# Row halves, fixed turns and an earlier pool mix in a macaron block with RWKV-7 and pooling

## The chip, the cores and the metric

The kernel runs on one core of one Trainium2 chip. TensorE (PE) multiplies matrices into PSUM, VectorE (DVE), ScalarE (ACT) and GpSimd (POOL) work elementwise, SyncE (SP) and POOL issue DMA transfers. Every engine works through its own queue in order and waits for others on semaphores. The metric is the device time of one execution in microseconds (us): the median of three runs was 2127.09, from 2125.59 to 2128.98. A difference of about 0.2% can be told from none.

## What is computed

One block on 256 tokens of width 2048, in float32, with about 400 MB of weights that are read once:

```python
def _swiglu(x, w_gate, w_up, w_down):
    return (jax.nn.silu(x @ w_gate) * (x @ w_up)) @ w_down

f = _swiglu(_rmsnorm(h, ln_ffn1_pre[l]), ffn1_gate[l], ffn1_up[l], ffn1_down[l])
h = h + MACARON_WEIGHT * _rmsnorm(f, ln_ffn1_post[l])
mx = _hybrid_mixer(_rmsnorm(h, ln_mix_pre[l]), ...)
h = h + _rmsnorm(mx, ln_mix_post[l])
f = _swiglu(_rmsnorm(h, ln_ffn2_pre[l]), ffn2_gate[l], ffn2_up[l], ffn2_down[l])
h = h + MACARON_WEIGHT * _rmsnorm(f, ln_ffn2_post[l])
```

The hidden width of both feed-forwards is 5632. The mixer multiplies by w_in, runs an RWKV-7 scan over 16 heads on one part of the result and four causal pooling windows (each followed by a 256 x 256 matrix, the "mix") on another, gates the two projected branches with sigmoids of the rest, and multiplies the sum by w_out.

## The kernel before

**Products.** Each float32 operand is split into a high and a low float32r part, and a product is three matmuls: high x high, high x low, low x high (`mm3`, lines 117 to 121). Activations are the stationary operand, 128 x 128 for one k-tile and one of two row halves (h = 0, 1: tokens 0 to 127, 128 to 255); weights are the moving operand, 512 columns wide. `load_w` (line 87) fetches two k-tiles of weights per DMA (512 KB, issued by SP), ACT casts them to the high part wH (L101), and DVE subtracts to get the low part wL (L102). There are four buffers for raw weights and five each for wH and wL, so weights run at most five pairs of k-tiles ahead.

**`gemm_tok`** (line 123) makes 512 columns of a product: normally for each k-tile both row halves in turn, each into its own PSUM bank, then the evacuation `evac(h, ps)`. With `lead` the first 10 k-tiles (STAG) go by row halves: all ten for h = 0, then all ten for h = 1. With `trail` the last 10 do, and each half is evacuated when it ends. The product that starts a stage is a lead, the last column block of a stage is a trail.

**`post`** (line 295) ends a stage: four column blocks of the down or output product. Each block's evacuation takes the sum of squares on ACT (L267) and multiplies by the norm's gain on DVE (L314). After the last block the sum is finished (L327), POOL raises it to the power -0.5 (L330), and DVE scales each of the four column blocks and adds the residual (L335, one step per row half and column block). Each finished block goes to `emit`, which stores it (a spill to DRAM by POOL, or the output by SP) and, between stages, calls the `emit` of `next_pre` (line 346): four PE transposes (L234), their split into xH on ACT (L240) and xL on DVE (L241) as the next stage's input, the block's sum of squares for the next norm (L267), and after four blocks the row's factor (`rstd`, L214 to L219).

**Order.** Tile, the framework, plans each engine's queue ahead of time, by simulated times and a priority that follows the program's order; `high_priority(offset)` moves instructions forward by so many places. Weight casts and most evacuations stand in `high_priority(offset=BOOST)`, 2000. Inside `manual_schedule(engines={PE})` PE takes its instructions exactly as the program gives them. Before the change only the mixer's middle part does so (line 578): there `weave` puts the scan's steps among the matmuls of the projections (`rest`), by estimated times (MM, MC: us per matmul).

**The pool branch.** `p_g` (line 519) makes four window products and the mix of each one window later; then a gate product of 32 steps (`gb_g(1)`, one step is a k-tile and a row half), and after it the mix of the fourth window (`pool_mix(3, ...)`). The window's evacuation ends with mxT, the input of the mix (L625 high, L626 low part); the mix's evacuation gives yb (L638 high, L639 low part), of which the projection `pb_g(0)` needs the fourth for its last two k-tiles.

**Buffers.** 33 units of 4 KB per partition hold activations. At the end of a feed-forward 22 of them are its hidden activations (hT), two are gains (gb), four the result (fg), four the residual; the next input takes eight. A unit comes free after its last reader.

Of the kernel before, what the change touches and what calls it, by code (L numbers as in the profile page):

```python
# [10 lines left out]
F32R = mybir.dt.float32r  # L11
# [5 lines left out]
P = 128  # L17
# [15 lines left out]
W32_BUFS = 4  # L33
WS_BUFS = 5
BOOST = 2000
MM, MC = 0.2265, 0.12
NUNITS = 33
STAG = 10
TB = 4

ROWS = [("ln_mix_pre", 16), ("ln_ffn2_pre", 16), ("mu", 26), ("w0", 8), ("a0", 8),
# [4 lines left out]
class Block:  # L46
    def __init__(s, tc, ctx):
        s.tc = tc
        s.nc = nc = tc.nc
        E = ctx.enter_context  # L50
        s.n = 0
        s.cp = E(tc.tile_pool(name="cp", bufs=1))
        s.wp = E(tc.tile_pool(name="wp", bufs=3))
        s.up = E(tc.tile_pool(name="up", bufs=NUNITS))
        s.tp = E(tc.tile_pool(name="tp", bufs=TB))
        s.sp = E(tc.tile_pool(name="sp", bufs=4))
        s.dp = E(tc.tile_pool(name="dp", bufs=1, space=bass.MemoryType.DRAM))
        s.pm = E(tc.tile_pool(name="pm", bufs=4, space=PSUM))
        s.pt = E(tc.tile_pool(name="pt", bufs=4, space=PSUM))
        s.ident = s.const([P, P], "ident")  # L60
        make_identity(nc, s.ident)
        s.mhalf = s.const([P, 16], "mhalf")
        nc.gpsimd.memset(s.mhalf, -0.5)
# [20 lines left out]
    def psum(s, p="pt"):  # L84
        return s.pt.tile([P, 512], F32, tag="pt", name=s.nm(p))

    def load_w(s, w, k0, nk, c0, cw, split=False):
        nc = s.nc
        out = []
        step = 1 if split else max(1, 1024 // cw)  # L90
        for j in range(k0, k0 + nk, step):
            n = min(step, k0 + nk - j)
            w32 = s.wp.tile([P, 1024], F32, tag="w32", name=s.nm("w32"), bufs=W32_BUFS)
            wH = s.wp.tile([P, 1024], F32R, tag="wH", name=s.nm("wH"), bufs=WS_BUFS)
            wL = s.wp.tile([P, 1024], F32R, tag="wL", name=s.nm("wL"), bufs=WS_BUFS)
            v, vH, vL = [t[:, :n * cw].rearrange("p (k c) -> p k c", k=n)
                         for t in (w32, wH, wL)]
            nc.sync.dma_start(out=v, in_=w[j * P:(j + n) * P, c0:c0 + cw]
                              .rearrange("(k p) c -> p k c", p=P))
            with s.tc.high_priority(offset=BOOST):  # L100
                nc.scalar.copy(vH, v)  # L101
                nc.vector.tensor_tensor(out=vL, in0=v, in1=vH.bitcast(F32), op=ALU.subtract)  # L102
            for i in range(n):
                out.append((j + i, vH[:, i], vL[:, i]))
        return out
# [17 lines left out]
    def gemm_tok(s, w, c0, at, KT, evac, lead=False, trail=False, first=False):  # L123
        pss = [s.pm.tile([P, 512], F32, tag="mm", name=s.nm("mm")) for _ in range(2)]

        def do(k, wH, wL, h):
            xH, xL = at(k)
            s.mm3(pss[h], xH[:, h * P:h * P + P], xL[:, h * P:h * P + P], wH, wL,
                  k == 0, k == KT - 1)

        k0 = 0
        while k0 < KT:
            nk = 4
            if lead and k0 == 0 or trail and k0 + STAG == KT:
                nk = STAG
            elif trail and KT - STAG - k0 < 4:
                nk = max(KT - STAG - k0, 2)
            nk = min(nk, KT - k0)
            stag = (lead and k0 == 0) or (trail and k0 + nk == KT)
            ws = []  # L140
            for k1 in range(k0, k0 + nk, 4):
                ws += s.load_w(w, k1, min(4, k0 + nk - k1), c0, 512, first and k1 == 0)
                if not stag:
                    for k, wH, wL in ws:
                        do(k, wH, wL, 0)
                        do(k, wH, wL, 1)
                    ws = []
            if stag:
                for h in range(2):
                    for k, wH, wL in ws:  # L150
                        do(k, wH, wL, h)
                    if k0 + nk == KT:
                        evac(h, pss[h])
            k0 += nk
        if not trail:
            with s.tc.high_priority(offset=BOOST):
                for h in range(2):
                    evac(h, pss[h])

    def tok_g(s, w, c0, at, KT, evac):  # L160

# [133 lines left out]
    def post(s, wd, at, KT, gpost, fac, resid, emit, reload):  # L295
        nc = s.nc
        gb = [s.unit(p="gb") for _ in range(2)]
        fg = [[s.unit(p="fg") for _ in range(2)] for _ in range(2)]
        ss = [s.small(4, "ss") for _ in range(2)]

        def cc_(u, c):
            return u[c // 2][:, (c % 2) * 512:(c % 2) * 512 + 512]

        part = [None, None]
        rr = [None, None]
        kf = 1.0 / (D * fac ** 2)

        for c in range(4):
            def ev(h, ps):
                if h == 0 and c % 2 == 0:  # L310
                    nc.gpsimd.dma_start(out=gb[c // 2], in_=gpost[c * 512:c * 512 + 1024]  # L311
                                        .partition_broadcast(P))
                s.sumsq(ps, ss[h][:, c:c + 1])
                nc.vector.tensor_tensor(out=cc_(fg[h], c), in0=ps, in1=cc_(gb, c), op=ALU.mult)  # L314
                if c == 2 and h == 0:
                    reload()
                if c == 2:
# [9 lines left out]
                nc.vector.tensor_scalar(out=r2, in0=ss[h][:, 3:4], scalar1=kf,  # L327
                                        scalar2=part[h], op0=ALU.mult, op1=ALU.add)
                r = s.small(1, "rs", bufs=8)
                nc.gpsimd.tensor_tensor(out=r, in0=r2, in1=s.mhalf[:, :1], op=ALU.pow)  # L330
                rr[h] = r
                for hh, q in ([(0, 0), (0, 1)] if h == 0 else
                              [(1, 0), (1, 1), (0, 2), (0, 3), (1, 2), (1, 3)]):
                    o = cc_(fg[hh], q)
                    nc.vector.scalar_tensor_tensor(out=o, in0=o, scalar=rr[hh],  # L335
                                                   in1=resid(hh, q), op0=ALU.mult,
                                                   op1=ALU.add)
                    emit(hh, q, o)
            s.gemm_tok(wd, c * 512, at, KT, ev, trail=(c == 3))

    def next_pre(s, gT):
        uT = s.new_T(4)
        ss = [s.small(4, "ss2") for _ in range(2)]
        rs = [None, None]

        def emit(h, c, ap):
            s.transpose_split(ap, uT, c, h, gT)
            s.sumsq(ap, ss[h][:, c:c + 1])
            if c == 3:
                rs[h] = s.rstd(ss[h], D)  # L350
        return uT, rs, emit

    def setup_mixer(s, prm):
# [73 lines left out]
    def mixer(s, prm, uT, rs, resid, emit, gpost, reload):  # L427
# [91 lines left out]
        def p_g():  # L519
            mix = None  # L520
            for g, win in enumerate(POOL_WINDOWS):
                mxT = s.unit((P, 2, 2, S), F32R, "mxT")
                yield from s.pool_window(g, win, at, w_in, mxT)
                if g:
                    yield from s.pool_mix(g - 1, mix, prm["pool_w"], pT)
                mix = mxT
            yield None
            yield from gb_g(1)
            yield from s.pool_mix(3, mix, prm["pool_w"], pT)

        sga = []

# [456 lines left out]
def kernel(tc, x, ln_ffn1_pre, ln_ffn1_post, ffn1_gate, ffn1_up, ffn1_down,  # L989
# [11 lines left out]
    with ExitStack() as ctx:  # L1001
# [3 lines left out]
        def at_tok(u):  # L1005
            return lambda h, c: u[h][c // 2][:, (c % 2) * 512:(c % 2) * 512 + 512]
# [25 lines left out]
            return f  # L1032
        hsp = s.dp.tile([2, 2, P, D], F32, tag="hsp", name="hsp")

        def emit1(h, c, ap):
            pre2(h, c, ap)
# [7 lines left out]
        def emit2(h, c, ap):  # L1044
            pre3(h, c, ap)
# [4 lines left out]
        def emit(h, c, ap):  # L1050
            nc.sync.dma_start(out=out[0, h * P:h * P + P, c * 512:c * 512 + 512], in_=ap)
        s.ffn(ffn2_gate[0], ffn2_up[0], ffn2_down[0], uT3, rs3, ln_ffn2_post[0],
              at_tok(h2), emit, load_to(h2, lambda h: hsp[1, h]))


_INS = ["x", "ln_ffn1_pre", "ln_ffn1_post", "ffn1_gate", "ffn1_up", "ffn1_down", "ln_mix_pre",
# [29 lines left out]
```

## Time and profile before

| what | us |
|---|---|
| median of three runs | 2127.09 |
| the profiled execution's own time | 2125.91 |
| its span, first to last instruction | 2124.2 |
| PE busy | 2093.8 |
| DVE busy | 1257.3 |
| ACT busy | 1115.9 |
| POOL busy | 77.7 |

The profile shows the first feed-forward until about 735 us, the mixer until about 1386 us, and the second feed-forward. Its rows give a start in us from the span's start, a duration, the engine, the line (L102 is line 102 of the kernel), the operation, output and inputs, shapes and a count; in square brackets stands the idle time before it and what ended that. Matmuls are pipelined, so the start of the next row tells more than a matmul's own duration. The granted clock is the share of TensorE's full clock that its throttle let through.

### The profile page before, as it was taken

The page shows a single profiled execution, that of the slowest core. Times are in us where ns is not written, and L with a number is a line of the kernel's source. Part 1 is how long each engine was busy: PE and PEld are TensorE (multiplying, and loading weights), DVE is VectorE, ACT ScalarE, POOL GpSimd, SP SyncE. Part 2 cuts the span into 40 slices and gives each one's busy share as a digit, 9 for nine tenths or more (in the row PEclk, how much of TensorE's full clock was granted, in tenths as well). Part 3 has the DMA queues.
Part 4 walks back from the last instruction along what each step waited for, and adds up shares of the span by engine and source line. Part 5 has one row for each costly group of instructions (what it writes and reads, how often), then busy time and mean ns, then how long its engine had stood idle before and what let it go on. Part 6 is the DMA issues. An engine that isn't in the chain of part 4 may idle for free.

```text
span 2124.2 us, 28823 instructions
## 1 busy us (share of the span) xinstructions
PE 2093.8 (99%) x11077; PEld 1762.0 (83%) x11077; DVE 1257.3 (59%) x1588; ACT 1115.9 (53%) x1600; POOL 77.7 (4%) x169
## 2 busy tenths in 40 slices
PE   8999999999999999999999999999999999999998
PEld 6888888888888789979988788878888888888886
DVE  6556555555444555788789666475555555554444
ACT  6565555655444465465465444365655556554442
POOL 1000000000000100000210110010000000000000
PEclk9999999999999999999999999999999999999999
DMA  7666666567666656655456575666666665676664
GB/s 238 193 185 199 198 194 192 179 217 246 192 195 191 197 165 185 178 175 168 140 149 190 158 257 181 187 199 197 179 206 193 195 191 182 215 245 194 193 193 134
DMA packets 223604, 406.99 MB, mean 192 GB/s; under 512 B 13151, under 2 KB 49129, under 8 KB 223465
## 3 DMA queue, kind: packets, MB, share of 16 engines
q1 hardware_dynamic: 216937, 383.11, 59.5%
q0 software_dynamic: 6528, 22.02, 2.9%
q8 instruction: 87, 1.43, 0.3%
q14 instruction: 52, 0.43, 0.1%
HBM read 396.69 MB, written 8.39 MB: 191 GB/s over the span
## 4 chain that ended last, share of the span: by engine, by line
PE 95%; DVE 2%; issue 1%; ACT 1%; DMA 1%; SPq 0%; DVEq 0%; POOLq 0%; POOL 0%; ACTq 0%
PE mm L119 28%; PE mm L121 27%; PE mm L120 27%; PE mc L204 10%; DVE wL L102 1%; DMA w<-in_ffn_gate_dram 1%; DVE fg L335 0%; PE pA L809 0%; PE tr L234 0%; ACT wH L101 0%; PE pU L905 0%; PE pY L940 0%; PE pSa L917 0%; DMA w<-in_w_proj_b_dram 0%; ACT junk L267 0%
## 5 line engine op out<-in xcount | busy, mean ns | idle before, releaser
L102 DVE TENSOR_TENSOR wL<-w,wH 128x1024 fp32r<-128x1024 f32 (+2 forms) x734 | 884.3, 1212 | 768.2 <-ACT wH L101 766.8
L101 ACT CAST wH<-w 128x1024 fp32r<-128x1024 f32 (+2 forms) x734 | 760.1, 1042 | 856.3 <-PE mm L121 700.2
L119 PE MATMUL mm<-wH,xH 128*128 128x512 f32 x2496 | 977.6, 392 | 6.8 <-ACT xH L240 6.8
L121 PE MATMUL mm<-wH,xL 128*128 128x512 f32 x2496 | 973.4, 391 | 4.6 <-DVE xL L241 4.6
L120 PE MATMUL mm<-wL,xH 128*128 128x512 f32 x2496 | 972.9, 390 | 0.3 <-DVE wL L102 0.3
L119 PEld LDWEIGHTS mm<-wH,xH 128*128 128x128 f32 x2496 | 469.8, 188 | 107.2 <-ACT xH L240 9.9
L121 PEld LDWEIGHTS mm<-wH,xL 128*128 128x128 f32 x2496 | 469.7, 188 | 103.4 <-DVE xL L241 6.0
L120 PEld LDWEIGHTS mm<-wL,xH 128*128 128x128 f32 x2496 | 470.0, 188 | 96.4 <-DVE wL L102 0.7
L204 PE MATMUL mc<-xH,wH 128*128 128x256 f32 x560 | 159.8, 285 | 0.0
L204 PE MATMUL mc<-xH,wL 128*128 128x256 f32 x560 | 158.4, 283 | 0.0
L204 PE MATMUL mc<-xL,wH 128*128 128x256 f32 x560 | 158.4, 283 | 0.0
L260 ACT COPY x<-T 32x256 f32<-32x256 f32 x352 | 141.8, 403 | 3.9
L204 PEld LDWEIGHTS mc<-xH,wH 128*128 128x128 f32 x560 | 106.0, 189 | 0.9
L204 PEld LDWEIGHTS mc<-xH,wL 128*128 128x128 f32 x560 | 106.0, 189 | 0.2
L204 PEld LDWEIGHTS mc<-xL,wH 128*128 128x128 f32 x560 | 106.0, 189 | 0.1
L279 ACT ACTIVATE sg<-mm,rs 128x512 f32<-128x512 f32 x44 | 30.1, 689 | 20.6 <-PE mm L121 20.6
L280 DVE SCALAR_TENSOR_TENSOR sg<-mm,rs,sg 128x512 f32<-128x512 f32 x44 | 31.6, 751 | 12.4 <-ACT sg L279 12.3
L311 POOL DMA_DIRECT2D gb<-in_ln_ffn_post_dram x4 | 2.2, 562 | 925.5 <-DVE xL L264 892.2
L267 ACT ACTIVATE junk<-mm 128x512 bf16<-128x512 f32 x24 | 14.3, 595 | 34.5 <-PE mm L121 34.5
L314 DVE TENSOR_TENSOR fg<-mm,gb 128x512 f32<-128x512 f32 x24 | 16.5, 692 | 24.5 <-ACT junk L267 24.5
L285 DVE SCALAR_TENSOR_TENSOR sg<-mm,rs,sg 128x512 f32<-128x512 f32 x44 | 30.9, 743 | 0.0
L250 DVE STREAM_TRANSPOSE T<-sg 128x512 f32<-128x512 f32 x44 | 30.8, 701 | 0.0
(236 smaller groups left out, 1007.0 us busy)
## 6 DMA issues: line engine op xcount, KB each, us to landing
w<-in_ffn_up_dram SPq DMA_DIRECT2D x176, 512.0 KB
w<-in_ffn_down_dram SPq DMA_DIRECT2D x176, 512.0 KB
w<-in_ffn_gate_dram SPq DMA_DIRECT2D x174, 512.0 KB
w<-in_w_in_dram SPq DMA_DIRECT2D x128, 512.0 KB
w<-in_w_out_dram SPq DMA_DIRECT2D x32, 512.0 KB
w<-in_w_proj_b_dram SPq DMA_DIRECT2D x16, 512.0 KB
w<-in_w_proj_a_dram SPq DMA_DIRECT2D x16, 512.0 KB
hsp<-fg POOLq DMA_DIRECT2D x16, 256.0 KB, 4.8
```

The source lines that it names most:

```text
L101: nc.scalar.copy(vH, v)
L102: nc.vector.tensor_tensor(out=vL, in0=v, in1=vH.bitcast(F32), op=ALU.subtract)
L119: nc.tensor.matmul(ps, aH, bH, start=start, stop=False)
L120: nc.tensor.matmul(ps, aH, bL, start=False, stop=False)
L121: nc.tensor.matmul(ps, aL, bH, start=False, stop=stop)
L204: s.nc.tensor.matmul(o, lh, rh, start=one and n == 0, stop=k == KT - 1 and n == 2, skip_group_check=True)
L250: s.nc.vector.transpose(out=T1[:, h * 512:h * 512 + 512], in_=src)
L260: nc.scalar.copy(dst[q * 32:q * 32 + 32, :, :, i], src[i * 32:i * 32 + 32, :, :, q])
L279: nc.scalar.activation(out=sg, in_=ps, func=AF.Sigmoid, scale=rs[h])
L280: nc.vector.scalar_tensor_tensor(out=sg, in0=ps, scalar=rs[h], in1=sg, op0=ALU.mult, op1=ALU.mult)
L285: nc.vector.scalar_tensor_tensor(out=sig[h], in0=ps, scalar=rs[h], in1=sig[h], op0=ALU.mult, op1=ALU.mult)
L314: nc.vector.tensor_tensor(out=cc_(fg[h], c), in0=ps, in1=cc_(gb, c), op=ALU.mult)
```

## The change

Four things change.

1. A trail takes its last 16 k-tiles (TRAIL) by row halves instead of 10. Their weights are loaded ahead; the pairs after the first five go into six activation units instead of the weight buffers (`hold`). For the output product, 16 k-tiles are all of it.
2. From the first matmul of a trail's row halves to the end of the following lead's row halves, PE's order is that of the program. Each row half is evacuated in `high_priority(offset=FINISH)`, 4000, when it ends. Its four finished blocks are no longer turned at once: each is put on a list (`turns`) with a time after the half's end, and `by_half` issues its transposes ahead of the first k-tile at or behind that time, by PE's own estimated time, or at the latest ahead of the k-tile that needs it.
3. The sums of squares and the factor of the next norm are put on another list (`late`), which is worked off after the lead's row halves. This holds for the kernel's own input at the start too. The residual steps now go row half by row half in the order of columns; before, part of the first half's stood behind the second's.
4. In the pool branch the fourth mix comes after 22 of the 32 steps of the gate product.

```diff
+FINISH = 4000
+TRAIL = 16
+TURNS = [[3.8, 5.2, 6.8, 8.6], [4.2, 5.4, 8.8, 10.4]]
...
+            if hold:
+                wH, wL = s.unit(dt=F32R, p="kH"), s.unit(dt=F32R, p="kL")
...
+        def by_half(ws):
+            for h in range(2):
+                now = 0
+                for k, wH, wL in ws:
+                    while s.turns and (s.turns[0][0] <= now or s.turns[0][1] == (h, k // 4)):
+                        s.turns.pop(0)[2]()
+                    do(k, wH, wL, h)
+                    now += 3 * MM
+                s.turns = [(t - now, b, f) for t, b, f in s.turns]
+                if k == KT - 1:
+                    with s.tc.high_priority(offset=FINISH):
+                        evac(h, pss[h])
...
+        def held(k0, k1):
             ws = []
+            for k in range(k0, k1, 2):
+                ws += s.load_w(w, k, 2, c0, 512, first and k < 4, k - k0 >= STAG)
+            return ws
+
+        if trail:
+            both(0, KT - TRAIL)
+            ws = held(KT - TRAIL, KT)
+            s.held = s.tc.manual_schedule(engines={mybir.EngineType.PE})
+            s.held.__enter__()
+            by_half(ws)
+            return
+        if lead:
+            by_half(held(0, STAG))
+            if s.held:
+                s.held.__exit__(None, None, None)
+                s.held = None
+            while s.late:
+                s.late.pop(0)()
+        both(STAG if lead else 0, KT)
...
-                for hh, q in ([(0, 0), (0, 1)] if h == 0 else
-                              [(1, 0), (1, 1), (0, 2), (0, 3), (1, 2), (1, 3)]):
...
+                for q in range(4):
+                    o = cc_(fg[h], q)
+                    nc.vector.scalar_tensor_tensor(out=o, in0=o, scalar=r, in1=resid(h, q),
+                                                   op0=ALU.mult, op1=ALU.add)
+                    emit(h, q, o, TURNS[h][q])
...
+            def turn():
+                with s.tc.high_priority(offset=FINISH):
+                    s.transpose_split(ap, uT, c, h, gT)
+
+            def stat():
+                s.sumsq(ap, ss[h][:, c:c + 1])
+                if c == 3:
+                    rs[h] = s.rstd(ss[h], D)
+            s.late.append(stat)
+            if at is None:
+                turn()
+            else:
+                s.turns.append((at, (h, c), turn))
...
-            yield from gb_g(1)
+            gate = gb_g(1)
+            for t in itertools.islice(gate, 22):
+                yield t
             yield from s.pool_mix(3, mix, prm["pool_w"], pT)
+            yield from gate
```

More of the change, by code (lines that the diff above doesn't have):

```diff
@@ L51, in __init__ @@
         s.n = 0
+        s.late, s.turns, s.held = [], [], None
         s.cp = E(tc.tile_pool(name="cp", bufs=1))
@@ L85, in psum, with load_w @@
         return s.pt.tile([P, 512], F32, tag="pt", name=s.nm(p))
-    def load_w(s, w, k0, nk, c0, cw, split=False):
+    def load_w(s, w, k0, nk, c0, cw, split=False, hold=False):
         nc = s.nc
@@ L93, in load_w @@
             w32 = s.wp.tile([P, 1024], F32, tag="w32", name=s.nm("w32"), bufs=W32_BUFS)
-            wH = s.wp.tile([P, 1024], F32R, tag="wH", name=s.nm("wH"), bufs=WS_BUFS)
-            wL = s.wp.tile([P, 1024], F32R, tag="wL", name=s.nm("wL"), bufs=WS_BUFS)
+            if hold:
+                wH, wL = s.unit(dt=F32R, p="kH"), s.unit(dt=F32R, p="kL")
+            else:
+                wH = s.wp.tile([P, 1024], F32R, tag="wH", name=s.nm("wH"), bufs=WS_BUFS)
+                wL = s.wp.tile([P, 1024], F32R, tag="wL", name=s.nm("wL"), bufs=WS_BUFS)
             v, vH, vL = [t[:, :n * cw].rearrange("p (k c) -> p k c", k=n)
@@ L129, in do @@
                   k == 0, k == KT - 1)
[L131 to L139, printed above, removed]
-            ws = []
[L141 to L158, printed above, removed]
+        def by_half(ws):
[10 more added lines that the diff above has]
+                        evac(h, pss[h])
@@ new lines, in both @@
+        def both(k0, k1):
+            for k2 in range(k0, k1, 4):
+                for k, wH, wL in s.load_w(w, k2, min(4, k1 - k2), c0, 512):
+                    do(k, wH, wL, 0)
+                    do(k, wH, wL, 1)
+        def held(k0, k1):
+            ws = []
+            for k in range(k0, k1, 2):
[8 more added lines that the diff above has]
+            return
@@ L160, in tok_g @@
+        if lead:
[6 more added lines that the diff above has]
+        both(STAG if lead else 0, KT)
+        with s.tc.high_priority(offset=BOOST):
+            for h in range(2):
+                evac(h, pss[h])
     def tok_g(s, w, c0, at, KT, evac):
@@ L330, in ev @@
                 nc.gpsimd.tensor_tensor(out=r, in0=r2, in1=s.mhalf[:, :1], op=ALU.pow)
-                rr[h] = r
-                for hh, q in ([(0, 0), (0, 1)] if h == 0 else
-                              [(1, 0), (1, 1), (0, 2), (0, 3), (1, 2), (1, 3)]):
[L334 to L338, printed above, removed]
+                for q in range(4):
[3 more added lines that the diff above has]
+                    emit(h, q, o, TURNS[h][q])
             s.gemm_tok(wd, c * 512, at, KT, ev, trail=(c == 3))
@@ L344, in next_pre, with emit @@
         rs = [None, None]
[L346 to L350, printed above, removed]
+        def emit(h, c, ap, at=None):
+            def turn():
[8 more added lines that the diff above has]
+                turn()
+            else:
+                s.turns.append((at, (h, c), turn))
         return uT, rs, emit
@@ L1033, with emit1 @@
         hsp = s.dp.tile([2, 2, P, D], F32, tag="hsp", name="hsp")
-        def emit1(h, c, ap):
-            pre2(h, c, ap)
+        def emit1(h, c, ap, at):
+            pre2(h, c, ap, at)
             nc.gpsimd.dma_start(out=hsp[0, h, :, c * 512:c * 512 + 512], in_=ap)
@@ L1042, with emit2 @@
         h2 = [[s.unit(p="h2") for _ in range(2)] for _ in range(2)]
-        def emit2(h, c, ap):
-            pre3(h, c, ap)
+        def emit2(h, c, ap, at):
+            pre3(h, c, ap, at)
             nc.gpsimd.dma_start(out=hsp[1, h, :, c * 512:c * 512 + 512], in_=ap)
@@ L1048, with emit @@
                 load_to(h1, lambda h: hsp[0, h]))
-        def emit(h, c, ap):
+        def emit(h, c, ap, at):
             nc.sync.dma_start(out=out[0, h * P:h * P + P, c * 512:c * 512 + 512], in_=ap)
@@ L1053 @@
               at_tok(h2), emit, load_to(h2, lambda h: hsp[1, h]))
+        s.held.__exit__(None, None, None)
 _INS = ["x", "ln_ffn1_pre", "ln_ffn1_post", "ffn1_gate", "ffn1_up", "ffn1_down", "ln_mix_pre",
```

1 line of the change is left out of this document (removed).

## The prediction

> **What bounds the kernel now.** I read the page's engine line first, then the waits of PE (waiter, releaser, total us, times, longest), then the chain that ended last, then busy time by stretch, and last the order in time of the few microseconds around each wait.
>
> ```profile
> PE 2093.8 (99%) x11077; PEld 1762.0 (83%) x11077; DVE 1257.3 (59%) x1588; ACT 1115.9 (53%) x1600; POOL 77.7 (4%) x169
> ...
> PE mm L119 <- ACT xH L240: 6.8, 7, 1.7
> PE mm L121 <- DVE xL L241: 4.6, 2, 2.4
> PE mm L121 <- DVE yb L639: 3.2, 1, 3.2
> ...
> PE pS L925 <- ACT R L919: 0.9, 1, 0.9
> ```
>
> PE is the bound, 99% busy. No number of matmuls changes here, so only time in which PE waits or runs slowly can be won. The waits name two kinds of place: matmuls on the split of a new input (xH, xL), and one on a pool result (yb). Busy time by stretch (us, then PE, PEld, DVE, ACT, POOL busy and instructions, granted clock, DMA share, GB/s) shows what they cost:
>
> ```profile
> 735.00:760.00 25.00, 20.60 (x88) 16.11 (x87) 20.31 (x51) 18.20 (x53) 6.92 (x26) 0.80 0.52 181
> 1385.80:1410.00 24.20, 19.52 (x92) 15.03 (x91) 19.68 (x45) 17.90 (x51) 5.69 (x9) 0.93 0.62 210
> ...
> 747.00:749.00 2.00, 2.00 (x6) 1.52 (x6) 1.88 (x8) 1.67 (x7) 1.10 (x15) 0.50 0.15 61
> ...
> 960.00:1370.00 410.00, 409.09 (x3066) 347.43 (x3065) 298.87 (x497) 206.48 (x294) 38.11 (x62) 1.00 0.59 180
> ```
>
> ```profile
> 1359.63 0.39 PE L120 MATMUL mm<-wL,xH 128*128 128x512 f32 x1
> ...
> 1377.54 0.39 PE L121 MATMUL mm<-wH,xL 128*128 128x512 f32 x1
> ```
>
> ```profile
> 752.89 1.31 PE tr L234 x12
> ```
>
> Between the two matmul rows lie 79 steps: 0.2267 us each at full clock. Twelve transposes on the chain take 1.31 us, 0.109 each. The two stretches are the boundaries (down of the first feed-forward into the mixer; output product into the second). Each holds 32 transposes (8 blocks of 4), so 56 and 60 matmuls. They would need 56 x 0.2267 + 32 x 0.109 = 16.2 us and 17.1 us; they took 25.0 and 24.2. So 8.8 and 7.1 us are lost, of which some 0.7 each is the change between transposes and matmuls and stays: 8.1 + 6.4 = **14.5 us** can be won there. It is more than the idle time, because the granted clock falls to 0.50 after it.
>
> What makes PE wait at a boundary, in order of time:
>
> ```profile
> 740.81 0.80 PE L121 MATMUL mm<-wH,xL 128*128 128x512 f32 x1 [2.37 <-DVE xL L241]
> ```
>
> ```profile
> 735.15 3.49 DVE L102 TENSOR_TENSOR wL<-w,wH 128x1024 fp32r<-128x1024 f32 x3
> ...
> 739.28 1.22 DVE L102 TENSOR_TENSOR wL<-w,wH 128x1024 fp32r<-128x1024 f32 x1
> 740.41 0.61 DVE L241 SCALAR_TENSOR_TENSOR xL<-tr,cols,xH 128x128 fp32r<-128x128 f32 x2
> ```
>
> The transposes come only when the old product has ended, and on DVE the split of the first block stands behind three weight splits (L102) and the evacuation of the second row half.
>
> **The change, part by part.** *Ends of down and output.* With 16 k-tiles by row halves, the second half lasts 16 x 3 x 0.2267 = 10.88 us instead of 6.80, and the first half's four blocks are turned inside it, at 3.8, 5.2, 6.8 and 8.6 us. The second half's blocks come inside the next product's first 10 k-tiles (6.80 us per half), at 4.2, 5.4, 8.8 and 10.4. PE's order is then fixed, so a late block stops it. How early is a block? The final product shows the chain alone, the first boundary shows it with a weight split inside:
>
> ```profile
> 2109.20 0.62 PE L121 MATMUL mm<-wH,xL 128*128 128x512 f32 x2
> ```
>
> ```profile
> 2109.63 0.60 ACT L267 ACTIVATE junk<-mm 128x512 bf16<-128x512 f32 x1 [6.88 <-PE mm L121]
> ```
>
> ```profile
> 2111.25 0.56 POOL L330 TENSOR_TENSOR rs<-rt,mhalf 128x1 f32<-128x1 f32 x1 [234.23 <-DVE rt L327]
> ```
>
> ```profile
> 2111.84 2.74 DVE L335 SCALAR_TENSOR_TENSOR fg<-fg,rs,h 128x512 f32<-128x512 f32 x4 [0.68 <-POOL rs L330]
> ```
>
> ```profile
> 729.70 0.60 ACT L267 ACTIVATE junk<-mm 128x512 bf16<-128x512 f32 x1 [6.88 <-PE mm L121]
> ```
>
> ```profile
> 732.50 2.73 DVE L335 SCALAR_TENSOR_TENSOR fg<-fg,rs,xr 128x512 f32<-128x512 f32 x4
> ```
>
> ```profile
> 739.45 1.47 POOL L330 TENSOR_TENSOR rs<-rt,mhalf 128x1 f32<-128x1 f32 x1 [3.38 <-DVE rt L327]
> ```
>
> The half's last slot ends at 2109.20 + 0.23 = 2109.43. ACT starts 0.20 later, DVE's first residual step (L335) 2.21 after ACT, and each takes 0.68: the first block is ready 0.20 + 2.21 + 0.68 = 3.1 us after the half, the others at 3.8, 4.5 and 5.1. With one weight split in between it is 2.80 instead of 2.21: 3.7, against the place at 3.8. The power on POOL (L330) took 1.47 beside a weight split and 0.56 alone, 0.9 more: 4.6, 0.8 late. So the first half's wait is 0 to 0.8 us; I take 0.5. For the second half ACT can be in a cast or a sum of squares (up to 1.0) as well, DVE in one more split (1.2): 3.1 to 6.2 against 4.2, a wait of 0 to 2.0; I take 0.8, since the chain seen with a split comes to 3.7. Later blocks have 1.4 us of room or more. Sum per boundary: 1.3 us of new waits (0 to 2.8), too short for the slow clock: the 0.9 us wait of pS lies in the stretch 960 to 1370, whose clock is 1.00. So 14.5 - 2.6 = **11.9 us** won, between 14.5 and, with waits of 2.8 and 1.5 us lost to a half-clock stretch after each (measured below at the pool's wait), 5.9.
>
> Here a page speaks for milder waits: the Trainium skill, "TensorE: Matmul & The Clock Gate", Part 1, has the clock halved only after an idle window of about 3.4 us. This trace differs, with 0.50 after waits of at most 2.4 us; by the page the worst end would be 8.9 instead of 5.9. Against the change speaks "SBUF — State Buffer", section "Who interferes with whom": a DVE operation with two SBUF inputs holds off a GpSimd operation that reads SBUF. The 1.47 us agree; it would make every first block 0.8 late.
>
> *Behind it.* Of the 8 weight pairs of the last 16 k-tiles, 3 lie in six other buffers, whose room comes from the down product's own inputs as its k-tiles end; cost 0 (if late: one pair's split, 1.2 us). POOL's spill writes go out with the blocks, before the second half's power needs POOL, and SP keeps its order of loads. The sums of squares (8 ACT steps) and the two powers behind them move past the next product's lead: they are needed only at that product's evacuation, some 8 us of matmuls later (6 k-tiles x 6 x 0.2267); cost 0. DVE is fuller: from the end of the first half it has some 5 weight splits, the evacuation and 16 block splits of 0.27, about 13.8 us of work in 10.9 us; what spills over is weights, of which five pairs are needed only over the next 6.8 us. Cost 0 to 1.2 us, inside the second half's range.
>
> *The start.* Squares and powers also leave the start's front, and the input's turns overtake weight casts there.
>
> ```profile
> 15.29 0.50 PE L119 MATMUL mm<-wH,xH 128*128 128x512 f32 x1 [1.65 <-ACT xH L240]
> ```
>
> ```profile
> 13.93 1.04 ACT L101 CAST wH<-w 128x1024 fp32r<-128x1024 f32 x1 [1.49 <-DMA w<-in_ffn_gate_dram]
> ```
>
> The longest wait there would end 0.3 us earlier at best, as its weights came by DMA at 13.93 and were cast by 14.97. A cast put back by splits costs about 1.0. I take 0, from +1.0 to -1.5. *The very end* keeps its last chain after the last matmul: 0.
>
> *The pool's last mix* goes from after the 32 steps of the gate product to after 22 of them.
>
> ```profile
> 927.09 0.39 PE L119 MATMUL mm<-wH,xH 128*128 128x512 f32 x1
> ...
> 949.57 0.50 PE L121 MATMUL mm<-wH,yb 128*128 128x512 f32 x1 [3.19 <-DVE yb L639]
> ...
> 951.87 0.63 PE L120 MATMUL mm<-wL,yb 128*128 128x512 f32 x1
> ...
> 954.14 2.22 PE L809 MATMUL pA<-R,R 64*128 64x128 f32 x32
> ```
>
> ```profile
> 930.01 0.42 DVE L626 TENSOR_TENSOR mxT<-pl,mxT 128x256 fp32r<-128x256 f32 x1
> ...
> 949.03 0.48 DVE L639 SCALAR_TENSOR_TENSOR yb<-mc,cols,yb 128x256 fp32r<-128x256 f32 x1
> ```
>
> The wait of 3.19 us goes, and with it the half-clock stretch to 954.14, worth about 1.5 (five matmuls take 2.27 us before that row instead of 1.13, and two ahead of them are slow too): 4.7 us. But step 23 begins at 927.09, and the mix's ninth matmul, 0.96 us on, needs the second low half of mxT, which DVE finished only at 930.43: unless DVE's order moves it, a new wait of 2.4 us, with or without the slow clock (1.5) after it. Gain between 0.8 and 4.7; I take **1.5**, as DVE's order ahead of that row does not hang on the mix.
>
> Sum: 11.9 + 0 + 1.5 = 13.4 us, against the profiled execution's own time of 2125.91 (span 2124.2, and 1.7 around it): 2112.5. That execution lies 1.2 us under the median of 2127.09; the forecast stands against its own time, so the gain to the median may read 14.6.
>
> **The rivals.** (1) *The mix waits for nothing*: with the pool weights ahead of the gate's last two pairs, DVE takes the mxT split earlier. Then 4.7 instead of 1.5: 2109.3. Against it: the row at 930.01. (2) *Turns late, the wait changes its name*: the new order stops PE for the residual step (L335) instead of the splits. With the worst ends above, 5.9 + 0.8 = 6.7 us won: 2119.2. For it: DVE's three splits in a row. Against: the evacuation now ranks above them. (3) *Slower*: PE's fixed order is hit again and again. A block that misses its place behind DVE's queue costs 2.4 us as at 740.81 and about 1.5 of half clock, 3.9 in all. With six of the sixteen blocks so, 23.4 us are lost against the 14.5 + 1.5 = 16.0 that the change wins without new waits at the boundaries: 2133.3. It decides from five blocks on, which eat the whole gain. Against it: only the first block of a half has under 1.4 us of room. (4) *It doesn't do what it says*: buffers for the held weights or the turned inputs come free only when the old product ends, and the turns slide back to where they are: 2126.
>
> **How the numbers follow.** Forecast 0.58, (1) 0.13, (2) 0.11, (4) 0.07, (3) 0.11. About 0.2%, 4.3 us, can be told from no change. Faster: the forecast, (1) and (2), 0.82; same: (4), 0.07; slower: (3), 0.11. The range from 2105.5 (every term at its good end, 14.5 + 4.7 + 1.0) to 2121 (rival 2 with the start's loss) leaves out (3) and (4).
>
> **What would show it.** Right: the waits of mm on xH and xL shrink from 6.8 + 4.6 = 11.4 to under 3.5 us; transposes stand in groups of 4 among matmuls of the old and the new product; the clock at the boundaries is 1.00; the wait on yb is gone and one on mxT of about 2.4 us stands near 928. Wrong: transposes waiting on fg (L335 after the change) for more than 1 us each, or matmuls on wL. The prediction fails most easily if DVE's order at the boundaries puts weight splits ahead of the chain of a half.

## The result, and the profile after

The changed kernel took 2121.72 us (median of 11 runs, 2120.01 to 2122.8) against 2127.2 us before (11 runs, 2124.72 to 2129.12): ratio 0.9974, 95% interval 0.9964 to 0.9983. It is 5.5 us faster. The forecast was 13.4 us faster than the profiled execution, 2112.5 us, and the range ended at 2121: the direction was right, the size was not. (Against the median of before the forecast was 14.6 us.) One of the ten executions of run e4 below took 4253.54 us, twice the others, and is left out of its figures.

The waits of PE after the change (waiter, releaser, total us, times, longest):

```profile
PE mm L126 <- ACT xH L263: 6.7, 4, 2.8
PE mm L128 <- DVE xL L264: 4.4, 3, 2.1
...
PE mc L227 <- DVE mxT L657: 1.8, 1, 1.8
```

L263 and L264 are the high and low split that were L240 and L241 before. The waits on xH and xL come to 11.1 us, against 11.4 before: as good as nothing went. (3.3 of these stand at the kernel's start, before the change 2.4; the rest at the two boundaries.) The wait on yb is gone, and one on mxT of 1.8 us is new.

For a balance by stage three kinds of row serve as marks in both kernels: the first sum of squares on the last down product's first row half (the entry to the first boundary), the pn matmuls (times of the first and the last), and the first pA. Two fences with the kernel before, then two with the changed one:

```profile
729.70 0.60 ACT L267 ACTIVATE junk<-mm 128x512 bf16<-128x512 f32 x1 [6.88 <-PE mm L121]
```

```profile
L726 PE MATMUL pn<-bones,R x32: 165/251/252, 915.3 to 1089.0; 128*128 128x2 f32 x32
...
L809 PE MATMUL pA<-R,R x128: 271/272/539, 954.1 to 1138.8; 64*128 64x128 f32 x128
```

```profile
725.68 0.60 ACT L290 ACTIVATE junk<-mm 128x512 bf16<-128x512 f32 x1 [5.43 <-PE mm L128]
```

```profile
L757 PE MATMUL pn<-bones,R x32: 165/252/252, 914.9 to 1085.6; 128*128 128x2 f32 x32
...
L840 PE MATMUL pA<-R,R x128: 271/272/374, 950.9 to 1135.4; 64*128 64x128 f32 x128
```

With halves of 16 k-tiles the first half ends 6 k-tiles earlier than with halves of 10, and 6 x 3 x 0.2267 = 4.08, so the entry is to be compared with 729.70 - 4.08 = 725.62. Start: 0.1 us later. First boundary: 915.3 - 725.62 = 189.7 against 189.2, 0.5 won. Pool's last mix: 954.1 - 915.3 = 38.8 against 36.0, 2.8 won. From pA to the last pn: 0.2. From there to the end of the spans (2124.2 and 2120.5), which holds the second boundary: 0.3. Sum 3.7 us, the difference of the two spans. So the two boundaries, which should have given 11.9 us, gave 0.8, and the pool gave more than its 1.5.

PE at the first boundary of the changed kernel:

```profile
729.57 0.60 PE L257 MATMUL tr<-ident,fg 128*128 128x128 f32 x4
731.40 0.60 PE L257 MATMUL tr<-ident,fg 128*128 128x128 f32 x4
733.91 0.60 PE L257 MATMUL tr<-ident,fg 128*128 128x128 f32 x4
735.74 0.60 PE L257 MATMUL tr<-ident,fg 128*128 128x128 f32 x4
742.44 0.50 PE L126 MATMUL mm<-wH,xH 128*128 128x512 f32 x1 [1.69 <-ACT xH L263]
745.24 0.80 PE L128 MATMUL mm<-wH,xL 128*128 128x512 f32 x1 [2.06 <-DVE xL L264]
```

```profile
745.00:750.00 5.00, 4.76 (x12) 3.69 (x13) 2.28 (x11) 2.07 (x8) 2.72 (x20) 0.50 0.44 157
740.00:750.00 10.00, 6.21 (x16) 4.18 (x16) 6.85 (x21) 7.07 (x25) 4.98 (x24) 0.72 0.48 162
```

The transposes of the first half's four blocks (four each, x4 in the rows) stand where the change puts them, inside the old product, and wait for nothing. Yet a piece of the split of these blocks is still missing when the next product reads it at 742, and again at 745, 6.7 and 9.5 us after the last block's transposes began. After the two waits the granted clock is 0.50. On DVE and ACT in that stretch:

```profile
730.55 3.49 DVE L109 TENSOR_TENSOR wL<-w,wH 128x1024 fp32r<-128x1024 f32 x3
733.96 0.34 DVE L264 SCALAR_TENSOR_TENSOR xL<-tr,cols,xH 128x128 fp32r<-128x128 f32 x1
734.22 1.22 DVE L109 TENSOR_TENSOR wL<-w,wH 128x1024 fp32r<-128x1024 f32 x1
735.35 0.86 DVE L264 SCALAR_TENSOR_TENSOR xL<-tr,cols,xH 128x128 fp32r<-128x128 f32 x3
737.93 1.23 DVE L109 TENSOR_TENSOR wL<-w,wH 128x1024 fp32r<-128x1024 f32 x1 [1.72 <-ACT wH L108]
...
741.92 2.74 DVE L355 SCALAR_TENSOR_TENSOR fg<-fg,rs,xr 128x512 f32<-128x512 f32 x4 [0.43 <-POOL rs L352]
744.58 0.86 DVE L264 SCALAR_TENSOR_TENSOR xL<-tr,cols,xH 128x128 fp32r<-128x128 f32 x3
```

```profile
730.73 0.35 ACT L263 ACTIVATE xH<-tr,cols 128x128 fp32r<-128x128 f32 x1
731.60 1.06 ACT L108 CAST wH<-w 128x1024 fp32r<-128x1024 f32 x1 [0.52 <-PE mm L128]
732.55 0.36 ACT L263 ACTIVATE xH<-tr,cols 128x128 fp32r<-128x128 f32 x1
734.55 0.62 ACT L263 ACTIVATE xH<-tr,cols 128x128 fp32r<-128x128 f32 x2 [1.63 <-PE tr L257]
736.85 1.05 ACT L108 CAST wH<-w 128x1024 fp32r<-128x1024 f32 x1 [1.67 <-DMA w<-in_w_in_dram]
737.80 1.13 ACT L263 ACTIVATE xH<-tr,cols 128x128 fp32r<-128x128 f32 x4
```

The splits come one to five at a time, between weight splits and the residual steps, and DVE idles for 1.72 us (before 737.93) while splits are outstanding. A full DVE doesn't look like that. (It idles for ACT's cast of the next weights, which itself waits 1.67 us for their DMA. By that cast ACT has done 4 of the first half's 16 pieces; the others stand behind it in ACT's queue.) A block is split in four pieces, and the code gives each piece to ACT (high) and then to DVE (low) before it goes to the next. ACT has one piece of a block at 730.73 and turns to a cast and another block. My reading, which the experiments put to the test: its next piece comes only when DVE has been at the one before, and DVE is three weight splits away from it. ACT's own waits have a row for this:

```profile
ACT xH L263 <- DVE xL L264: 5.4, 12, 1.0
```

Only 0.5 us of it lies ahead of PE's waits at the first boundary; there the chain shows less as idle time of ACT than as pieces that stand late in its queue.

### The profile page after: what moved, and what is told of

It is laid out like the page before. It is cut to its first block, busy times and chain, and to the rows that moved or that the text cites. A ratio compares the mean times of both kernels' runs of the same rounds, so it can differ in the third digit from the quotient of the medians.

```text
span 2120.5 us, 28818 instructions
## 1 busy us (share of the span) xinstructions
PE 2091.8 (99%) x11077; PEld 1761.7 (83%) x11077; DVE 1256.8 (59%) x1588; ACT 1117.5 (53%) x1600; POOL 76.2 (4%) x169
## 4 chain that ended last, share of the span: by engine, by line
PE 76%; issue 20%; DVE 1%; DMA 1%; ACT 1%; POOL 1%; POOLq 0%; DVEq 0%; SPq 0%; ACTq 0%
PE mm L126 21%; PE mm L128 21%; PE mm L127 21%; PE mc L227 10%; DMA w<-in_ffn_gate_dram 1%; PE pA L840 0%; DVE fg L355 0%; DMA mb<-msp 0%; PE tr L257 0%; ACT x L283 0%; PE pU L936 0%; PE pY L971 0%; PE pSa L948 0%; PE pY L967 0%; PE pM L906 0%
## 5 line engine op out<-in xcount | busy, mean ns | idle before, releaser
L109 DVE TENSOR_TENSOR wL<-w,wH 128x1024 fp32r<-128x1024 f32 (+2 forms) x725 | 872.9, 1211 | 750.2 <-ACT wH L108 748.7
L108 ACT CAST wH<-w 128x1024 fp32r<-128x1024 f32 (+2 forms) x725 | 751.2, 1043 | 833.3 <-PE mm L128 675.6
L126 PE MATMUL mm<-wH,xH 128*128 128x512 f32 x2460 | 965.8, 393 | 6.8 <-ACT xH L263 6.7
L128 PE MATMUL mm<-wH,xL 128*128 128x512 f32 x2460 | 961.6, 391 | 4.4 <-DVE xL L264 4.4
L127 PE MATMUL mm<-wL,xH 128*128 128x512 f32 x2460 | 959.5, 391 | 0.0
L126 PEld LDWEIGHTS mm<-wH,xH 128*128 128x128 f32 x2460 | 463.8, 189 | 104.2 <-ACT xH L263 8.5
L128 PEld LDWEIGHTS mm<-wH,xL 128*128 128x128 f32 x2460 | 463.9, 189 | 102.4 <-DVE xL L264 6.1
L127 PEld LDWEIGHTS mm<-wL,xH 128*128 128x128 f32 x2460 | 463.9, 189 | 94.2
```

What stands on the lines that cost most here:

```text
L126: nc.tensor.matmul(ps, aH, bH, start=start, stop=False)
L127: nc.tensor.matmul(ps, aH, bL, start=False, stop=False)
L128: nc.tensor.matmul(ps, aL, bH, start=False, stop=stop)
```

## The experiments

**Theory A**: the alternation of ACT and DVE within a block ties ACT's pieces to DVE's queue, and this took the gain. **Theory B**: DVE has too much to do in the second half (three weight splits ahead, 16 block splits), whatever the order. Times are medians, ratios are to the kernel before (2127.2 to 2127.4 in these groups of runs). The runs were made in three groups: e1, e3, e4, e6; then e7 to e10; then e11 and e12. They are told here by what they test.

**e1: four high splits, then four low ones**, everywhere.

```
             for i in range(4):
                 g = gT[:, j * 4 + i:j * 4 + i + 1]
                 nc.scalar.activation(out=dH[:, i], in_=ps[:, i], func=AF.Copy, scale=g)
+            for i in range(4):
+                g = gT[:, j * 4 + i:j * 4 + i + 1]
                 nc.vector.scalar_tensor_tensor(out=dL[:, i], in0=ps[:, i], scalar=g, ...
```

> Edit: the changed kernel, with the four ACT pieces of a block's split given first and the four DVE pieces behind them, instead of one and one in turn. Theory A (the turn-by-turn order: every ACT piece waits for the DVE piece before it, so that one DVE piece planned behind weight splits holds the whole block): at both boundaries the waits of mm on xH and xL, 1.69 + 2.06 us, fall under 1 us together and the half-clock stretch behind them goes; about 4 us of waits and 2 us of slow clock less at each boundary, some 10 to 12 us in all: 2110 to 2112. Theory B (DVE is simply full there: about 13.8 us of work in 10.9): the same DVE work in another order ends as late, the waits stay above 3 us per boundary, and the time stays within 1.5 us of the changed kernel's 2121.7.

2108.18 us (2107.31 to 2108.62), 0.9913, interval 0.9897 to 0.993: 13.5 us faster than the changed kernel, with the same instructions, and a little under the 2110 to 2112 of theory A. DVE at the first boundary:

```profile
729.62 3.49 DVE L109 TENSOR_TENSOR wL<-w,wH 128x1024 fp32r<-128x1024 f32 x3
733.02 1.12 DVE L266 SCALAR_TENSOR_TENSOR xL<-tr,cols,xH 128x128 fp32r<-128x128 f32 x4
```

The three weight splits still stand ahead of the first block, but now the block follows in one piece, and the clock in 730 to 760 is 1.00. Theory B falls.

**e9: the same only in the blocks turned at the boundaries**; the start's blocks keep the alternation.

```
-                    s.transpose_split(ap, uT, c, h, gT)
+                    s.transpose_split(ap, uT, c, h, gT, at is not None)
```

> The change, with the four high splits ahead of the four low ones only in the blocks turned at stated places, so at the two boundaries; the start's blocks keep the alternation. Theory A (the alternation at the boundaries took the gain): 9 to 12 us of the 13.5 that the edit won everywhere come from here: 2109.5 to 2112.5 us, granted clock 1.00 in 730 to 760 and in 1380 to 1410, waits on xH and xL under 3 us beside those of the start. Rival (most of what the edit won lies at the start): 2115 to 2119, with the start's first gate product 4 us or more earlier in the edit everywhere than here.

2108.6 us (2108.32 to 2108.96), 0.9913, interval 0.9899 to 0.9926, just under theory A's range. No matmul waits for xH or xL at a boundary. The stretch of the first boundary in the changed kernel, and then in e9 (us, then PE, PEld, DVE, ACT, POOL busy and instructions, granted clock, DMA share, GB/s):

```profile
730.00:760.00 30.00, 26.21 (x116) 20.69 (x115) 21.45 (x47) 19.83 (x53) 6.21 (x27) 0.89 0.50 161
```

```profile
730.00:760.00 30.00, 29.78 (x146) 24.38 (x145) 24.77 (x56) 22.27 (x61) 6.62 (x27) 1.00 0.63 199
```

PE issues 146 matmuls and transposes there instead of 116. Nearly all of what e1 won lies at the boundaries. ACT in e9:

```profile
730.59 1.13 ACT L266 ACTIVATE xH<-tr,cols 128x128 fp32r<-128x128 f32 x4
731.60 1.06 ACT L108 CAST wH<-w 128x1024 fp32r<-128x1024 f32 x1
732.54 1.17 ACT L266 ACTIVATE xH<-tr,cols 128x128 fp32r<-128x128 f32 x4
734.42 1.15 ACT L266 ACTIVATE xH<-tr,cols 128x128 fp32r<-128x128 f32 x4 [0.70 <-PE tr L257]
737.03 1.05 ACT L108 CAST wH<-w 128x1024 fp32r<-128x1024 f32 x1 [1.46 <-DMA w<-in_w_in_dram]
```

The cast waits for its DMA here as well, 1.46 us, but 12 pieces stand ahead of it instead of 4. So the late weights are not what held the splits back.

**e11 and e12: why ACT waits for DVE.** In e11 the alternation stays, but each block at the boundaries is turned twice, into two PSUM banks, and DVE reads the second. In e12 the turns are doubled too, but both engines read the first bank and the second is not read (`pL = ps` in place of `pL = p2`).

```
+        pL = ps
+        if two:
+            p2 = s.psum("tr2").rearrange("p (k t) -> p k t", k=4)
+            for i in range(4):
+                nc.tensor.transpose(p2[:, i], src[:, i * P:(i + 1) * P], s.ident)
+            pL = p2
...
-                nc.vector.scalar_tensor_tensor(out=dL[:, i], in0=ps[:, i], scalar=g,
+                nc.vector.scalar_tensor_tensor(out=dL[:, i], in0=pL[:, i], scalar=g,
```

> The change with its alternation of high and low splits kept, but each of the 16 blocks turned at the boundaries is turned twice, into two PSUM banks: ACT reads one, DVE the other. That is 64 transposes more, 64 x 0.109 = 7.0 us of PE. Theory (a high split waits for the low split before it because both read one bank): the waits of ACT on xL at the boundaries go, the waits of matmuls on xH and xL there are under 1 us, and the time is that of the split order at the boundaries, 2108.6, plus 7.0: 2115.6 (2114 to 2118). Rival (the alternate order by itself, or DVE's weight splits, hold the splits back, whatever bank they read): 2121.7 + 7.0 = 2128.7 (2126 to 2131).

> The control of the run before: the same doubled transposes into two PSUM banks, but ACT and DVE both read the first, and the second is not read. Both theories: 2121.7 + 7.0 = 2128.7 (2126 to 2131), with waits on xH and xL of about 2 us and a half clock at both boundaries as in the change. If it is below 2120, the doubled transposes themselves changed the order of the work, and the comparison says nothing of banks.

e11: 2121.86 us (2118.78 to 2122.49), 0.9974. e12: 2127.03 us (2125.28 to 2128.05), 1.0001. The control's time lies in its range, and e11 came 5.2 us lower, but not at 2115.6. The control's waits were not those expected: at the boundaries it is the transposes that wait for DVE's reads, and the matmuls' waits on xH stand at the start alone. The waits of ACT and of PE in e12:

```profile
ACT xH L269 <- DVE xL L270: 7.3, 13, 1.0
...
PE tr L262 <- DVE xL L270: 6.8, 2, 3.7
PE mm L126 <- ACT xH L269: 3.3, 2, 2.8
```

In e11 no row of ACT's xH waiting for DVE's xL is left, and DVE has a block's four pieces at once again (its waits of PE, then DVE):

```profile
PE tr L262 <- ACT xH L269: 3.7, 2, 1.9
...
PE mm L126 <- ACT xH L269: 2.4, 3, 1.7
```

```profile
733.21 1.12 DVE L270 SCALAR_TENSOR_TENSOR xL<-tr,cols,xH 128x128 fp32r<-128x128 f32 x4
```

(The matmuls' 2.4 us on xH in e11 lie at the start, none at a boundary.) So ACT's waits hang on the shared bank: same instructions, same order of writing, another bank for DVE, and they are gone. Of the 6.3 us that e11 missed, 3.7 have their own row, transposes that wait for ACT's read (1.78 and 1.94 us, one at each boundary); in its profiled execution the pool won 1.5 less than in e9, and the rest is not taken apart. A likely reason for the transposes' waits, not tested: four blocks of two banks each, where the pool of these tiles has four banks. I had not reckoned with that.

**e7: the kernel before with the split order of e1 alone.**

> The kernel before, with one edit: a block's four high splits on ACT are written first, then its four low splits on DVE. No row halves of 16, no stated turns, the pool as before. Theory A (the alternation costs time at a boundary whether or not the turns are moved, and the moved turns are worth most of the 14.5 us by themselves): a part of the waits on xH and xL goes, some 1 to 3 us at each boundary and 0 to 2 us at the start: 2119 to 2125 us; the transposes still stand behind the end of the old product, and the granted clock still falls in 735 to 760. Rival (the order of the splits is all that counts, and row halves and turns are worth nothing): 2108 to 2112, as low as the change with the same edit, 2108.2.

2122.38 us (2120.24 to 2123.58), 0.9978, interval 0.9968 to 0.9988: 4.9 us. The waits at the boundary stay, because the turns still stand behind the old product's end:

```profile
740.10 0.80 PE L121 MATMUL mm<-wH,xL 128*128 128x512 f32 x1 [2.37 <-DVE xL L243]
```

The change on top of this order is worth 2122.38 - 2108.18 = 14.2 us; on the alternate order it was 5.5. The rival, that the order is all that counts, falls.

**e10: e1 with row halves of 10 k-tiles** (TRAIL = 10), places of the turns as they are.

> The change with the four high splits first everywhere, and with 10 k-tiles by row halves at the end of a product in place of 16, so that the second half lasts 6.8 us and not 10.9; the places of the turns as they are, so the first half's third and fourth block come inside the next product's lead. Theory A (DVE was never full, only its order was bad): 2108 to 2111 us, at most one wait of about 1 us more at each boundary. Rival (the longer half is what gives DVE the room for three weight splits and 16 block splits): waits on xL of 2 us and more with a half clock behind them are back at both boundaries, 2113 to 2120.

2112.19 us (2111.54 to 2114.03), 0.9931, interval 0.9916 to 0.9946: 4.0 us slower than e1, and neither number fits. At the first boundary PE waits three times, at the second likewise (0.53, 1.04, 0.47), at a clock of 1.00 throughout:

```profile
736.99 0.50 PE L128 MATMUL mm<-wH,xL 128*128 128x512 f32 x1 [0.52 <-DVE xL L266]
743.45 0.66 PE L257 MATMUL tr<-ident,fg 128*128 128x128 f32 x4 [0.91 <-DVE fg L357]
747.82 0.50 PE L128 MATMUL mm<-wH,xL 128*128 128x512 f32 x1 [0.47 <-DVE xL L266]
```

These are 1.90 + 2.04 = 3.9 us, where e1 waits 0.34 + 1.02 = 1.36 at the boundaries: about 2.6 of the 4.0 us are such waits, the rest is not taken apart. With the turns at these places the longer half is worth 4.0 us.

**e3: the start as before the change**, squares and powers back in the start's front.

> Edit: the changed kernel, but the kernel's own input at the start is turned, squared and summed as before the change (no higher priority, no later sums). Theory A (the start's new order costs the 1.2 us by which the first gate product ends later, 34.62 instead of 33.42): it ends at 33.4 again, and the time falls by 1.2 to about 2120.5. Theory B (the 0.17 us later landing of the fourth pair of weights does it, run by run): it ends at 34.4 or later, and nothing changes.

2121.13 us (2119.96 to 2124.51), 0.9973, interval 0.9964 to 0.9983, not apart from the changed kernel. Its first gate product ends at 35.0 us, not at the 33.4 of theory A: nothing shows that the start's new order took back part of the gain.

**e4: the kernel before with the pool's move alone. e8: the change without it.**

> Edit: the kernel before, with only the pool's last mix moved to after 22 of the gate's 32 steps. Theory A (the mix's part is worth what the changed trace shows: 3.2 us of wait and 1.5 of half clock go, 1.8 of wait on mxT come): 2.9 us less, about 2124.3, with a wait on mxT of 1.8 to 2.4 us and none on yb. Theory B (the gain hangs on what the other parts do to DVE's order ahead of it): the wait on mxT is longer with half clock behind it, and the gain is under 1 us.

> The change without the move of the pool's last mix, so the ends and the start alone. The change as a whole gained 5.5 us on the medians. If the pool's move is worth what the two traces show beside each other (2.8 us between the pn row and the first pA row), the ends and the start together gained 2.7: 2124.5 us (2123.5 to 2125.5), and the wait on yb of about 3 us is back. If it is worth only what it gave on the kernel before (1.0 us, 2126.4 against 2127.4), the ends gained 4.5: 2122.8 (2122 to 2123.5).

e4: 2125.98 us (2124.35 to 2127.28), 0.9994, interval 0.9985 to 1.0004. e8: 2125.42 us (2122.74 to 2126.27), 0.9989, interval 0.998 to 0.9998. So the move gives 1.4 us (within what can be told from nothing, and between the two theories) on the kernel before, and 2125.42 - 2121.72 = 3.7 us inside the change, and the ends and the start alone give 1.8. The two pool rows, first the changed kernel with the ninth product matmul behind it, then e4 with the first:

```profile
929.59 0.51 PE L227 MATMUL mc<-mxT,wH 128*128 128x256 f32 x2 [1.79 <-DVE mxT L657]
...
932.00 0.40 PE L128 MATMUL mm<-wH,xL 128*128 128x512 f32 x1
```

```profile
931.48 0.58 PE L204 MATMUL mc<-mxT,wH 128*128 128x256 f32 x2 [1.79 <-DVE mxT L629]
932.29 0.63 PE L119 MATMUL mm<-wH,xH 128*128 128x512 f32 x1
```

The wait is the same 1.79 us, but in e4 it is followed by matmuls of 0.63 us until 934.9 (granted clock 0.97 in 905 to 960), in the changed kernel it isn't (1.00). From the first pn to the first pA, e4 won 1.2 us and the changed kernel 2.8; the half-clock stretch is that difference of 1.6. It does not hang on the pool's move alone: with the same wait, e11 and e12 have such a stretch, e1, e3, e9 and e10 have none.

**e6: e1, the start as before, and the pool's mix after 26 steps** in place of 22.

> Edit: the changed kernel with three edits together: the split of a block with its four ACT pieces first, the start as before the change, and the pool's last mix after 26 of the 32 steps instead of 22. Theory A: the sum of its parts, 10 to 12 us at the boundaries, 1.2 at the start and 1.8 in the pool (no wait on mxT and none on yb): 2107 to 2109. Theory B: the start and the pool alone, 3.0: 2118.7.

2107.54 us (2106.84 to 2107.6), 0.9911, interval 0.9896 to 0.9926: 0.6 us under e1 and the lowest here, though their spreads overlap. The wait on mxT is gone, and one of 1.0 us on the pool's weights (wL) stands in its place.

By the marks above, won against the kernel before (us, profiled executions; halves of 10 k-tiles are compared with 729.70, those of 16 with 725.62):

| kernel | start | boundary 1 | pool | pA to pn | boundary 2, end | sum |
|---|---|---|---|---|---|---|
| changed | -0.1 | 0.5 | 2.8 | 0.2 | 0.3 | 3.7 |
| e8 without pool | 0.5 | 0.3 | 0.0 | 0.2 | 0.2 | 1.2 |
| e9 split order at the boundaries | 0.1 | 7.5 | 2.7 | 0.2 | 7.1 | 17.6 |
| e1 split order everywhere | 0.9 | 7.4 | 2.7 | 0.2 | 6.1 | 17.3 |
| e10 split order, 10 k-tiles | 1.4 | 4.9 | 2.8 | 0.2 | 4.2 | 13.5 |
| e7 before, split order | 0.7 | 2.4 | -0.2 | 0.2 | 0.5 | 3.6 |
| e4 before, pool moved | -1.8 | 0.3 | 1.2 | 0.2 | -1.2 | -1.3 |
| e11 two banks | 0.7 | 2.4 | 1.2 | 0.2 | 0.1 | 4.6 |
| e12 two turns, one bank | 0.2 | -1.0 | 1.1 | 0.2 | -0.9 | -0.4 |

e11 and e12 have 32 transposes more at each boundary, 32 x 0.109 = 3.5 us. Even so the second bank alone is worth 3.4 us at the first boundary and 1.0 at the second.

## Why the prediction was right or wrong

*What can be won, 14.5 us.* Right. e9 won 7.5 + 7.1 = 14.6 at the two boundaries, with PE at full clock.

*The first half's chain and the turns.* Right: the transposes of a first half's four blocks came at their places without a wait. The second half's blocks were not the trouble either; in e9 the first of them waits 0.2 us for the residual step, against 0.8 taken.

*Behind it: "some 5 weight splits, the evacuation and 16 block splits of 0.27, about 13.8 us of work in 10.9 us; what spills over is weights. Cost 0 to 1.2 us".* This step failed, and it is the whole miss at the boundaries: 11.9 us forecast, 0.8 measured, so that 13.7 of the 14.5 us stayed lost instead of 2.6. I added up DVE's time as if the 16 low splits were independent and ranked ahead. They are chained with ACT's: piece by piece, high, low, high, low, and each high split has to wait for the low one before it, which queues behind a weight split (1.22 us, or 3.49 for three) or the residual steps (2.74). What spilled over was splits of the next product's input, not weights. The bad end of 5.9 us didn't hold it, since it priced late transposes alone. The trace of before showed the chain, in the waits of ACT; the prediction used the waits of PE alone and left this row out:

```profile
ACT xH L240 <- DVE xL L241: 11.2, 8, 2.9
```

The Trainium skill, "PSUM — Partial Sum Buffer", section "PSUM bank collisions raise a hardware error", says that the compiler's scheduler makes any two instructions of different engines on one bank and the same partitions depend on each other, two reads as well. The runs agree with such a dependency: 7.3 us of such waits with one bank (e12), none with two (e11). Whether that scheduler set it here, no run shows.

*The sums of squares, "move past the next product's lead; cost 0".* The cost was right, the place was not: ACT took the eight at 740.5 to 746.5, inside the lead and among the pieces of the splits. In e9 they stand there too (739.6 to 747.9), without a wait on a split.

*The start, 0 (from +1.0 to -1.5).* Right as far as can be told: -0.1 in the balance, and e3 makes no difference. Its spread is larger than the term: e4, whose start is that of before, came 1.8 us later to its first boundary. The good end of 1.0 did not follow from the row shown for it, which gave 0.3 at best, and with it the range's lower end adds up to 2105.7, not 2105.5.

*The pool's mix, 1.5 (0.8 to 4.7).* The mechanism was right: the wait on yb goes, a wait on mxT comes. The size was off: 1.79 us instead of 2.4, and in the profiled execution no half clock behind it, so 2.8 won. It cannot be taken as fixed: e4, e11 and e12 got the half clock after the same wait, so its absence was luck.

*Rival 2, "turns late, the wait changes its name" (2119.2).* It came nearest in time, but not in cause: no transpose waits for the residual step (L355) there, and the waits kept their old names. *Rivals 1, 3 and 4*: the mix does wait, nothing got slower, and the turns don't slide back. *What would show it*: waits on xH and xL of less than 3.5 us and a clock of 1.00 are what e9 shows at the boundaries (no such wait; 3.8 us at the start); the changed kernel showed 11.1 us in all and 0.50. The sentence on what would make the forecast fail, weight splits ahead of a half's chain, named the wrong victim: the chain of the half came through, the splits of the turned blocks didn't.

## What to carry to other kernels

Before moving work earlier, read what its *consumers on the helper engines* wait for: an engine at half load can still be late when its work is a chain of short steps that hands over to another engine's queue and back. Where two engines read one PSUM bank, write all steps of the one before those of the other. Giving each its bank took ACT's waits away too, but the doubled transposes ate the gain (e11, 2121.86 us). And a step counted as hidden needs an order, not only room: adding up busy time showed 13.8 us of work against 10.9, but neither that sum nor DVE's idle time decided, since the same instructions in another order were 13.5 us faster.

## What the runs showed of the hardware

- Where ACT and DVE only read, in different columns of one PSUM bank, the built program makes the later read wait for the earlier: ACT waited 13 times, 7.3 us, in e12, and not once with two banks (e11). I had not expected a wait between two reads. What the chip would do without this order, no run shows.
- The granted clock fell to 0.50 after two waits of 1.69 and 2.06 us with 745.24 - 2.06 - 742.44 = 0.7 us of matmuls between them. After a single wait of 1.78 to 1.81 us on mxT it fell in three kernels and stayed at 1.00 in five: in e4 the first matmuls behind the wait are slow, in e11 the slow ones begin 0.8 us after its end and in e12 1.3 us after it, and the changed kernel, e1, e3, e9 and e10 have none. Waits of 0.5 to 1.0 us (e10) left it at 1.00. The Trainium skill, "TensorE: Matmul & The Clock Gate", Part 1, has the clock halved after a window of about 3.4 us that runs freely, so that the phase counts. A free phase would fit the eight cases on mxT, a full idle window doesn't fit any of these waits, and no run here settles which rule holds.
- Parts of the program that are the same in both kernels differ by up to 1.8 us between two profiled executions (the start of e4 against that of before), so a term under 2 us that hangs on the start can't be read from one pair of traces.
